# A hybrid decoder layer on one core: bulk elementwise work put on VectorE, and tiles laid over other memory in the FFN and embedding stages

## The chip, the cores and the metric

The kernel runs on one core of a Trainium2 chip. The metric is the device time of one execution in microseconds (us), the median of several runs. The core has a matrix engine (TensorE, PE in the profile), three engines for elementwise work (VectorE or DVE, ScalarE or ACT, GpSimd or POOL) and SyncE (SP), on whose queue this kernel issues its DMAs.

## The reference, cut to what matters

One layer of a decoder, over 1056 tokens (32 of the decoding samples, then 1024 of a prompt), width 1024, float32. Every half has a norm ahead of it and a norm behind it, whose result is added to the residual:

```python
x += 0.5 * post(swiglu_1(pre(x)))                 # FFN1, inner width 2816
cols = pre(x) @ w_in
x += post(concat(gdn(cols), swa(cols)) @ w_out)   # gated DeltaNet and sliding-window attention
x += 0.5 * post(swiglu_2(pre(x)))                 # FFN2
x += post(sigmoid(x @ ple_gate) * (p @ ple_proj)) # per-layer input embedding ("PLE")

def swiglu(h, w_gate, w_up, w_down):
    return (silu(h @ w_gate) * (h @ w_up)) @ w_down
```

It also returns the convolution and recurrent states and the attention caches.

## The kernel before, in words

**Precision.** Every float32 operand is split into a rounded half `hi` and a rest `lo = x - hi`; a product is three matmuls (hi·hi, hi·lo, lo·hi; `mm3`, lines 136 to 138, `mm3p`, lines 353 to 355). A split is a cast on ScalarE and a subtraction, which for weights is line 129 (128x1024, tile `wsp` from `raw`), on VectorE unless the caller passes `pl`, and then on GpSimd.

**Tiling.** Activations lie with features on the partitions (8 slices of 128) and tokens along a row, in three chunks `CH` of 288, 384 and 384 tokens. Weights come in 1 MB raw tiles, two buffers, are split into units and used once for every chunk.

**Stages.** Load and pre-norm (`apply_norm`, lines 217 to 227: scale, cast to `hi`, subtraction for `lo` at line 226, odd slices on GpSimd). FFN up (`ffn_up`): the first and last weight groups directly, the groups between by a scheme of seven products for chunks 1 and 2 together, whose token-side sums come from `half_sums` (lines 359 to 377): four steps `k`, each four additions on GpSimd (line 366), four on VectorE (368 to 371), and three splits (375, 376; the first on GpSimd). The SwiGLU output is written to memory tile by tile (`scr_h<-sg`, line 399), 22 tiles of 128 features for each chunk. FFN down (`ffn_down`): for each chunk `load_g` reads the 22 tiles back one at a time (line 538, tile `gr`, four buffers) and splits them to `gt` (539, 540); the matmuls run over them; a `Sum` (lines 192 to 211: square on ScalarE, addition on an engine of a list) gathers the norm; and `finish`, a generator, does the post-norm, residual (610, 611) and the next stage's `hi`/`lo` of the chunk before, two of its steps behind each weight unit. Then come the input projection, the recurrent and attention groups (the "mixer"), the output projection (`load_mix` reads the mixed tiles `xm` and gates `zz`), FFN2 in the same way with chunk order 1, 2, 0, and PLE: gate matmuls (lines 1719 to 1723, in the order chunks 1, 2, 0), input tiles `pin`, their transposes to `pT`, the projection units `upj`, and a norm with `gB`.

**What sets the order.** The program is written stage by stage, and a scheduler with priorities orders each engine's instructions; each engine then runs its queue strictly in that order, and SP issues the DMAs in its own. Memory comes from pools that are opened and closed: a pool opened after another closed lies over the same bytes, and its first writes wait for the last uses of what lay there. `fp` holds FFN up's own tiles (the sums `st`, `ut`, the outputs `sg`); it is closed ahead of the down stage, whose pools `yd` (one output tile of 8x384) and `gp` (`gt` and `gr`) lie there. In PLE, `pp`, `pr` and `pe` lie over these in turn; the fourth gate unit is `u3`.

## Time and profile before

| | |
|---|---|
| median of 3 runs | 2448.47 us (2448.35 to 2451.45) |
| the profiled execution | 2444.39 us |
| its span, first to last instruction | 2442.7 us |
| mean granted TensorE clock | 0.963 of full |
| PE busy | 2265.5 us (93%) |
| VectorE, ScalarE, GpSimd busy | 1422.3, 924.3, 294.0 us |

The profile is one execution. A row of a group reads: line, engine, operation, output tile from input tiles, shapes, count; then busy time and the mean of one in ns; then how long the engine stood idle before these instructions and which instruction ended that. A timeline row has the start, the length, the instruction, and in brackets the idle time before it with what ended it. In a row of windows the busy times of PE, weight loads, VectorE, ScalarE and GpSimd follow the window's length, then the granted clock, the share of the DMA engines and GB/s.

### The profile page before, as it was taken

To read this page: it belongs to the slowest core of one execution; us is meant where nothing else is said; L and a number is where in the kernel's file an instruction comes from. 1 tells how busy PE (TensorE), PEld (TensorE's weight loads), DVE (VectorE), ACT (ScalarE), POOL (GpSimd) and SP (SyncE) were. 2 spreads that over 40 slices of the span, in tenths; PEclk is the share of its full clock that TensorE was granted. 3 is DMA by queue.
4 is the path that set the end of the run, shared out by engine and by line. 5 is a ranking of instruction groups with operands and counts; after the bars stand their busy time and mean duration, and the time that the engine had idled before them with its cause. 6 is when DMAs were issued, how large, how long until landed. Compare 5 with 4: busy or idle time off the path is not lost. (4 is left out here: it accounts for less than half of the span.)

```text
span 2442.7 us, 36595 instructions
## 1 busy us (share of the span) xinstructions
PE 2265.5 (93%) x14212; PEld 2153.6 (88%) x14212; DVE 1422.3 (58%) x2839; ACT 924.3 (38%) x1862; POOL 294.0 (12%) x303
## 2 busy tenths in 40 slices
PE   6899999979999598879999989899999989999798
PEld 5899999979999597878887888799999989999576
DVE  6755555545774548891456668855555554655425
ACT  5322223335453335423326644322223234444221
POOL 2400000000000225332110333500000000001000
PEclk9999999989999798989999988999999999999799
DMA  6122222266554425646554544122222265554201
GB/s 230 57 77 91 75 83 75 83 211 207 195 193 130 128 67 190 180 132 191 176 178 123 150 164 165 48 75 83 75 83 73 85 207 182 188 169 142 96 16 57
DMA packets 312915, 313.17 MB, mean 128 GB/s; under 512 B 26185, under 2 KB 295569, under 8 KB 312726
## 3 DMA queue, kind: packets, MB, share of 16 engines
q1 hardware_dynamic: 312742, 310.84, 39.4%
q8 instruction: 112, 1.84, 0.3%
q14 instruction: 61, 0.50, 0.1%
HBM read 235.57 MB, written 77.81 MB: 128 GB/s over the span
## 5 line engine op out<-in xcount | busy, mean ns | idle before, releaser
L129 DVE TENSOR_TENSOR wsp<-raw,wsp 128x1024 fp32r<-128x1024 f32 (+1 forms) x271 | 325.9, 1203 | 266.2 <-ACT wsp L128 265.3
L128 ACT CAST wsp<-raw 128x1024 fp32r<-128x1024 f32 (+1 forms) x290 | 293.5, 1015 | 310.4 <-PE mm L355 178.7
L353 PE MATMUL mm<-gt,wsp 128*128 128x384 f32 (+1 forms) x1056 | 342.8, 326 | 24.1 <-ACT gt L539 10.2
L355 PE MATMUL mm<-gt,wsp 128*128 128x384 f32 (+1 forms) x1056 | 342.4, 325 | 2.9 <-DVE wsp L129 2.9
L354 PE MATMUL mm<-gt,wsp 128*128 128x384 f32 (+1 forms) x1056 | 342.7, 325 | 0.0
L136 PE MATMUL mm<-hhi,wsp 128*128 128x384 f32 (+1 forms) x784 | 265.6, 339 | 14.9 <-ACT po L767 10.8
L138 PE MATMUL mm<-hhi,wsp 128*128 128x384 f32 (+1 forms) x784 | 263.3, 336 | 4.0 <-DVE wsp L129 2.3
L137 PE MATMUL mm<-hlo,wsp 128*128 128x384 f32 (+1 forms) x784 | 263.8, 336 | 0.7 <-DVE hlo L226 0.5
L353 PEld LDWEIGHTS mm<-gt,wsp 128*128 128x128 f32 x1056 | 200.9, 191 | 26.6 <-ACT gt L539 20.8
L353 PE MATMUL ax<-hhi,wsp 128*128 128x384 f32 x640 | 215.5, 337 | 0.1
L355 PE MATMUL ax<-hhi,wsp 128*128 128x384 f32 x640 | 215.1, 336 | 0.2 <-DVE wsp L129 0.2
L354 PE MATMUL ax<-hlo,wsp 128*128 128x384 f32 x640 | 215.2, 336 | 0.0
L355 PEld LDWEIGHTS mm<-gt,wsp 128*128 128x128 f32 x1056 | 201.2, 191 | 4.3 <-DVE wsp L129 3.9
L354 PEld LDWEIGHTS mm<-gt,wsp 128*128 128x128 f32 x1056 | 201.2, 191 | 1.6 <-DVE gt L540 1.0
L128 ACT CAST wsp<-st 128x1024 fp32r<-128x1024 f32 x80 | 84.3, 1054 | 278.3 <-PE ax L355 272.0
L353 PE MATMUL ax<-th,wsp 128*128 128x384 f32 x480 | 161.7, 337 | 15.1 <-ACT th L375 15.1
L136 PEld LDWEIGHTS mm<-hhi,wsp 128*128 128x128 f32 x784 | 154.4, 197 | 19.1 <-ACT po L767 12.3
L353 PE MATMUL mm<-hhi,wsp 128*128 128x288 f32 x576 | 169.9, 295 | 0.1
L354 PE MATMUL mm<-hlo,wsp 128*128 128x288 f32 x576 | 169.8, 295 | 0.0
L355 PE MATMUL mm<-hhi,wsp 128*128 128x288 f32 x576 | 169.5, 294 | 0.0
L354 PE MATMUL ax<-th,wsp 128*128 128x384 f32 x480 | 161.6, 337 | 1.6 <-POOL th L376 1.6
L355 PE MATMUL ax<-th,wsp 128*128 128x384 f32 x480 | 160.9, 335 | 0.0
(461 smaller groups left out, 4696.8 us busy)
## 6 DMA issues: line engine op xcount, KB each, us to landing
raw<-in_ffn_w_down_dram SPq DMA_DIRECT2D x48, 1024.0 KB
raw<-in_ffn_w_gate_dram SPq DMA_DIRECT2D x24, 1024.0 KB
raw<-in_ffn_w_up_dram SPq DMA_DIRECT2D x24, 1024.0 KB
raw<-in_ffn_w_down_dram SPq DMA_DIRECT2D x24, 768.0 KB
scr_h<-sg SPq DMA_DIRECT2D x88, 192.0 KB
gr<-scr_h SPq DMA_DIRECT2D x88, 192.0 KB
raw<-in_w_out_dram SPq DMA_DIRECT2D x12, 1024.0 KB
xr<-scr_x SPq DMA_DIRECT2D x12, 768.0 KB
```

Source lines behind the costliest of these rows:

```text
L128: S.copy(hi, src)
L129: (G if pl else V).tensor_tensor(lo, src, hi.bitcast(F32), ALU.subtract)
L136: TE.matmul(ps, lhsT=wh, rhs=xh, start=(i == 0), stop=False)
L137: TE.matmul(ps, lhsT=wh, rhs=xl, start=False, stop=False)
L138: TE.matmul(ps, lhsT=wl, rhs=xh, start=False, stop=(i == n - 1))
L353: TE.matmul(ps, lhsT=wh, rhs=xh, start=(first and i == 0), stop=False, skip_group_check=on)
L354: TE.matmul(ps, lhsT=wh, rhs=xl, start=False, stop=False, skip_group_check=on)
L355: TE.matmul(ps, lhsT=wl, rhs=xh, start=False, stop=(last and i == n - 1), skip_group_check=on)
```

## The change

1. Every large GpSimd subtraction or addition goes to VectorE: the `pl` splits (line 129, 19 instructions), the split at 784 (4), the odd `lo` slices of 226 (24), 626 and 1630 (12 each), the mixed tiles' `lo` (1510, 24), the additions of `half_sums` (366, 32, and 376, 8), and GpSimd's share of `Sum` (209, 18): 153 instructions. GpSimd keeps small operations of the mixer.
2. A pool `fq`, opened ahead of `fp`, takes `st` and `ut`; so `yd` of the down stage lies over these and no longer over output tiles. The first chunk of each down stage reads its first tiles (10 of 288 tokens, 8 of 384) in one DMA into a `yd` tile `ga`.
3. In PLE the pool order is turned: `pe` (now `y0b`, `gB`, `y1`) comes first, so that `pp` and `pr` (with `u3`, `upj`, `pin`, `pT`) lie over `gt`/`gr`. The load of `gB` moves to the second half.
4. In FFN2 down, `finish` takes four steps behind each weight unit (`rate`), FFN1 two as before.

```diff
-        (G if pl else V).tensor_tensor(lo, src, hi.bitcast(F32), ALU.subtract)
+        V.tensor_tensor(lo, src, hi.bitcast(F32), ALU.subtract)
...
-            (G if d % 2 else V).tensor_tensor(lo[:, d, :], hf, hi[:, d, :].bitcast(F32), ALU.subtract)
+            tt(lo[:, d, :], hf, hi[:, d, :].bitcast(F32), ALU.subtract)
...
-        s2 = Sum(n, "x", (G, V)) if sq else None
+        s2 = Sum(n, "x", (V,)) if sq else None
...
-                G.tensor_tensor(t, f32(hh[:, q, :]), f32(ll[:, q, :]), ALU.add)
+                tt(t, f32(hh[:, q, :]), f32(ll[:, q, :]), ALU.add)
...
-                (V if i else G).tensor_tensor(T[i][:, 1, k, :], t, f32(T[i][:, 0, k, :]), ALU.subtract)
+                V.tensor_tensor(T[i][:, 1, k, :], t, f32(T[i][:, 0, k, :]), ALU.subtract)
...
-            s12, s34 = [fp.tile([P, 1024], F32, name=nm("st"), tag="st", bufs=2) for _ in range(2)]
+            s12, s34 = [fq.tile([P, 1024], F32, name=nm("st"), tag="st", bufs=2) for _ in range(2)]
...
+            na = 0
+            if c == order[0]:
+                na = KT * 384 // n
+                ga = wide([P, KT, 384], F32, name=nm("ga"), tag="yd", bufs=1).rearrange("p a b -> p (a b)")[:, :na * n]
+                ga = ga.rearrange("p (f n) -> p f n", n=n)
+                dma(ga, scr[:, 0:na, c0:c0 + n])
             for f in range(NF):
                 gt = gp.tile([P, 2, 384], F32R, name=nm("gt"), tag="gt")[:, :, :n]
-                gr = gp.tile([P, 384], F32, name=nm("gr"), tag="gr", bufs=4)[:, :n]
-                dma(gr, scr[:, f, c0:c0 + n])
+                if f < na:
+                    gr = ga[:, f, :]
+                else:
+                    gr = gp.tile([P, 384], F32, name=nm("gr"), tag="gr", bufs=4)[:, :n]
+                    dma(gr, scr[:, f, c0:c0 + n])
...
-                        next(prev, None)
-                        next(prev, None)
+                        for _ in range(rate):
+                            next(prev, None)
...
-            G.tensor_tensor(lo, src, hi.bitcast(F32), ALU.subtract)
+            tt(lo, src, hi.bitcast(F32), ALU.subtract)
...
-            G.tensor_tensor(lo[:, k, :], xm, hi[:, k, :].bitcast(F32), ALU.subtract)
+            tt(lo[:, k, :], xm, hi[:, k, :].bitcast(F32), ALU.subtract)
...
-        ss = Sum(n, "y", (G, V))
+        ss = Sum(n, "y", (V,))
...
-            (G if d % 2 else V).tensor_tensor(lo[:, d, :], y[:, d, :], f32(hi[:, d, :]), ALU.subtract)
+            V.tensor_tensor(lo[:, d, :], y[:, d, :], f32(hi[:, d, :]), ALU.subtract)
...
+        y0b = pe.tile([P, 3, 512], F32, name="y0b")
+        gB = pe.tile([P, D], F32, name="gB")
         u3 = pp.tile([P, 2, 1024], F32R, name=nm("wsp"), tag="wsp")
...
-        gB = pr.tile([P, D], F32, name="gB")
-        dma(gB, A["norm_ple_post"].broadcast_to([P, D]))
-        V.tensor_scalar(gB, gB, 0.5, None, op0=ALU.mult)
         y0a = pr.tile([P, 6, 512], F32, name="y0a")
-        y0b = pe.tile([P, 3, 512], F32, name="y0b")
...
                 us = gate_units(1)
+                dma(gB, A["norm_ple_post"].broadcast_to([P, D]))
+                V.tensor_scalar(gB, gB, 0.5, None, op0=ALU.mult)
...
-                    y = pr.tile([P, 512], F32, name=nm("y1"), tag="y1", bufs=2)[:m]
+                    y = pe.tile([P, 512], F32, name=nm("y1"), tag="y1", bufs=2)[:m]
...
-    with tc.tile_pool(name="pp", bufs=1) as pp, tc.tile_pool(name="pr", bufs=1) as pr, tc.tile_pool(name="pe", bufs=1) as pe:
+    with tc.tile_pool(name="pe", bufs=1) as pe, tc.tile_pool(name="pp", bufs=1) as pp, tc.tile_pool(name="pr", bufs=1) as pr:
```

The scheduler reacts to these edits with another order at three places that matter here. On PE, in the first half-sum stage before, the matmuls of two successive sets of sums (`th`, accumulating in one `ax` tile, rows of the same unit) stand close together:

```order
392 L353 MATMUL ax_927<-th_814,wsp_910 128x384
393 L354 MATMUL ax_927<-th_814,wsp_910 128x384
394 L355 MATMUL ax_927<-th_814,wsp_910 128x384
395 L353 MATMUL ax_927<-th_814,wsp_910 128x384
396 L353 MATMUL ax_928<-hhi_557,wsp_910 128x384
```

On PE after (the same place; lines 353 to 355 are unchanged, and `mm_1121` and `ax_1104` belong to the next unit, `wsp_1086`):

```order
396 L355 MATMUL ax_930<-th_817,wsp_913 128x384
397 L355 MATMUL ax_931<-hhi_560,wsp_913 128x384
...
401 L353 MATMUL ax_1104<-hhi_392,wsp_1086 128x384
...
428 L355 MATMUL mm_1121<-hhi_208,wsp_1086 128x288
429 L353 MATMUL ax_930<-th_817,wsp_913 128x384
```

Matmuls of the next unit, 12 into `ax` and 24 into `mm` in this stretch and its continuation, have moved ahead of the later `th` matmuls.

On SP at the end of FFN1 up, before (`raw` are weights of the down stage, `sg` the last output tiles, `xr` residuals):

```order
114 L556 DMA raw_4642<-in_ffn_w_down_dram 128x8x256
...
116 L399 DMA scr_h_89<-sg_4406 128x288
117 L556 DMA raw_4698<-in_ffn_w_down_dram 128x6x256
...
119 L399 DMA scr_h_89<-sg_4460 128x288
...
121 L538 DMA gr_4473<-scr_h_89 128x288
122 L538 DMA gr_4478<-scr_h_89 128x288
```

After (line 540 is the new load, 547 the `gr` load, 565 the weights):

```order
114 L540 DMA ga_4476<-scr_h_89 128x10x288
115 L399 DMA scr_h_89<-sg_4409 128x288
116 L565 DMA raw_4628<-in_ffn_w_down_dram 128x8x256
117 L565 DMA raw_4684<-in_ffn_w_down_dram 128x6x256
118 L399 DMA scr_h_89<-sg_4463 128x288
...
120 L547 DMA gr_4509<-scr_h_89 128x288
```

The new load stands ahead of the two last output tiles, and the weight load that stood ahead of them now stands between them.

On ScalarE at the start of PLE, before (`hhi` are the last chunk's `hi` slices, `wsp_21411` is `u3`):

```order
1512 L597 COPY rb_21364<-fx_21337 128x288
1513 L1629 CAST hhi_21382<-yd_20592 128x288 x8
1514 L128 CAST wsp_21411<-raw_21323 128x1024
1515 L128 CAST upj_21418<-raw_21416 128x1024
1516 L128 CAST upj_21421<-raw_21416 128x1024
```

After (`u3` is `wsp_21389`; line 606 was 597, 1641 was 1629):

```order
1513 L128 CAST wsp_21389<-raw_21299 128x1024
1514 L1685 CAST identr<-cx 128x128
1515 L128 CAST upj_21396<-raw_21394 128x1024
1516 L128 CAST upj_21399<-raw_21394 128x1024
1517 L606 COPY rb_21340<-fx_21313 128x288
1518 L1712 CAST pT<-ax_21409 128x384
...
1521 L1641 CAST hhi_21358<-yd_20568 128x288 x2
```

The fourth gate unit, the projection units and the first `pT` have moved ahead of the last chunk's `hi` slices.

More of the change, by code (lines that the diff above doesn't have):

```diff
@@ L375, in half_sums, with ffn_up @@
                 S.copy(T[i][:, 0, k, :], t)
-                (V if i else G).tensor_tensor(T[i][:, 1, k, :], t, f32(T[i][:, 0, k, :]), ALU.subtract)
+                V.tensor_tensor(T[i][:, 1, k, :], t, f32(T[i][:, 0, k, :]), ALU.subtract)
             yield
     SGB = 10
-    def ffn_up(H, wg, wu, fp, scr, order, opent, hooks={}):
+    def ffn_up(H, wg, wu, fq, fp, scr, order, opent, hooks={}):
         NG = F // 256
@@ L510, in tmp @@
                 def tmp(self):
-                    return fp.tile([P, 384], F32, name=nm("ut"), tag="ut", bufs=4)
+                    return fq.tile([P, 384], F32, name=nm("ut"), tag="ut", bufs=4)
                 def c0(self, j, ps):
@@ L526, in ffn_up, with ffn_down @@
             classic(0, NG - 1, j, ug, uu)
-    def ffn_down(wd, gp, scr, order, yt, finish, after):
+    def ffn_down(wd, gp, scr, order, yt, finish, after, wide, rate):
         NF = F // 128
@@ L625, in g_pre_norm @@
             S.copy(hi[:, d, :], hf)
-            (G if d % 2 else V).tensor_tensor(lo[:, d, :], hf, f32(hi[:, d, :]), ALU.subtract)
+            V.tensor_tensor(lo[:, d, :], hf, f32(hi[:, d, :]), ALU.subtract)
             yield
@@ L633, in emit @@
     scr_h = [dram.tile([P, F // 128, T], F32, name=f"scr_h{i}") for i in range(2)]
+    fqc = tc.tile_pool(name="fq", bufs=1)
+    fq = fqc.__enter__()
     fpc = tc.tile_pool(name="fp", bufs=2)
@@ L655, in nx @@
         return f
-    ffn_up(H, A["ffn1_w_gate"], A["ffn1_w_up"], fp, scr_h[0], (0, 1, 2), open_t, hooks={
+    ffn_up(H, A["ffn1_w_gate"], A["ffn1_w_up"], fq, fp, scr_h[0], (0, 1, 2), open_t, hooks={
         (0, -1): nx(0), (0, 0): nx(1, 0), (0, 1): nx(1, 2), (0, 3): nx(1), (0, 4): nx(2, 2, 0, 1, 2),
@@ L661, in emit @@
     fpc.__exit__(None, None, None)
+    fqc.__exit__(None, None, None)
     w_in = A["w_in"][0]
@@ L688, in emit @@
         ffn_down(A["ffn1_w_down"], gp, scr_h[0], (0, 1, 2), lambda c: yd.tile([P, KT, 384], F32, name="yd", tag="yd", bufs=1) if c == 2
-                 else big.tile([P, KT, 384], F32, name=nm("yd"), tag="b2")[:, :, :CH[c][1]], finish1, first_units)
+                 else big.tile([P, KT, 384], F32, name=nm("yd"), tag="b2")[:, :, :CH[c][1]], finish1, first_units, yd.tile, 2)
     MGT, MLE = cm[:, 0:128], cm[:, 128:256]
@@ L1649, in emit @@
     ycur[0] = None
-    with tc.tile_pool(name="fp2", bufs=2) as fp:
-        ffn_up(H2, A["ffn2_w_gate"], A["ffn2_w_up"], fp, scr_h[1], (1, 2, 0), open_t)
+    with tc.tile_pool(name="fq2", bufs=1) as fq, tc.tile_pool(name="fp2", bufs=2) as fp:
+        ffn_up(H2, A["ffn2_w_gate"], A["ffn2_w_up"], fq, fp, scr_h[1], (1, 2, 0), open_t)
         tpc.pop().__exit__(None, None, None)
@@ L1654, in emit @@
         ffn_down(A["ffn2_w_down"], gp, scr_h[1], (1, 2, 0), lambda c: big.tile([P, KT, 384], F32, name=nm("yd"), tag="b2") if c == 1
-                 else yd.tile([P, KT, 384], F32, name=nm("yd"), tag="yd", bufs=1)[:, :, :CH[c][1]], finish2, first_gates)
+                 else yd.tile([P, KT, 384], F32, name=nm("yd"), tag="yd", bufs=1)[:, :, :CH[c][1]], finish2, first_gates, yd.tile, 4)
     def ple(pp, pr, pe):
```

## The prediction, made before the changed kernel was run

> **What bounds the kernel now.** I read the page's busy times first, then the whole span cut into stages.
>
> ```profile
> PE 2265.5 (93%) x14212; PEld 2153.6 (88%) x14212; DVE 1422.3 (58%) x2839; ACT 924.3 (38%) x1862; POOL 294.0 (12%) x303
> ```
>
> TensorE (PE) is the bound: 2265.5 of 2442.7 us, so 177 us are idle. The matmuls themselves do not change, so only idle time, and matmuls run at a reduced clock, can be won. In the stages the columns are the busy time of PE, PEld, VectorE (DVE), ScalarE (ACT) and GpSimd (POOL), then the granted clock:
>
> ```profile
> 505.00:556.00 51.00, 37.97 (x250) 36.75 (x249) 21.29 (x35) 19.95 (x37) 0.00 (x0) 0.87 0.75 242
> 800.00:843.00 43.00, 18.29 (x98) 15.58 (x98) 29.46 (x69) 13.88 (x28) 10.51 (x10) 0.68 0.45 143
> 843.00:1270.00 427.00, 391.85 (x2843) 356.88 (x2842) 267.22 (x788) 163.19 (x502) 119.52 (x157) 0.96 0.51 157
> 1400.00:1560.00 160.00, 141.82 (x810) 136.55 (x809) 119.41 (x241) 72.24 (x135) 59.64 (x46) 0.91 0.46 152
> 1560.00:1585.00 25.00, 16.38 (x84) 14.78 (x84) 23.60 (x30) 9.05 (x18) 15.01 (x12) 0.80 0.02 7
> 2200.00:2300.00 100.00, 77.45 (x496) 72.16 (x495) 53.51 (x89) 37.51 (x61) 12.67 (x8) 0.83 0.43 142
> ```
>
> The loss sits at transitions: FFN1 up to down (13.0 us idle), FFN1 down to input projection (24.7), recurrent mixer (35.2 in 427), output projection (18.2), half-sums (8.6), FFN2 down to embedding (22.6). What PE waited for, with total, times and longest:
>
> ```profile
> PE ax L353 <- ACT th L375: 15.1, 4, 6.0
> PE mm L1719 <- ACT wsp L128: 12.3, 1, 12.3
> PE fx L172 <- DVE ss L209: 12.1, 5, 4.8
> PE ax L1056 <- DVE qk L1069: 12.0, 4, 6.4
> PE mm L136 <- ACT po L767: 10.8, 2, 10.1
> PE fx L582 <- DVE ss L209: 10.7, 3, 9.7
> PE mm L353 <- ACT gt L539: 10.2, 3, 7.8
> PE mm L353 <- DMA gr<-scr_h: 9.3, 1, 9.3
> PE mm L353 <- ACT yd L568: 3.4, 1, 3.4
> ```
>
> A wait costs more than itself. These windows lie on the matmuls right behind such waits, and the granted clock there is a half:
>
> ```profile
> 103.60:109.20 5.60, 5.60 (x17) 5.16 (x18) 5.02 (x10) 3.34 (x8) 1.85 (x2) 0.50 0.00 0
> 1569.20:1580.30 11.10, 6.23 (x17) 5.03 (x18) 11.10 (x14) 3.08 (x6) 7.56 (x6) 0.54 0.01 2
> 527.80:532.40 4.60, 4.60 (x19) 4.60 (x20) 3.01 (x7) 2.59 (x6) 0.00 (x0) 0.50 0.59 166
> 542.70:546.10 3.40, 3.40 (x16) 3.40 (x16) 0.80 (x3) 0.29 (x1) 0.00 (x0) 0.50 1.03 355
> 2288.50:2300.50 12.00, 9.55 (x25) 6.64 (x26) 5.19 (x6) 3.60 (x6) 0.00 (x0) 0.50 0.71 240
> ```
>
> Half of the busy time in such a window is lost: 2.8, 3.1, 2.3, 1.7 and 4.8 us.
>
> **The change part by part.** *The moved elementwise work.* 153 instructions leave GpSimd. What they took there, and the like of them on VectorE:
>
> ```profile
> L129 POOL TENSOR_TENSOR wsp<-raw,wsp 128x1024 fp32r<-128x1024 f32 x19 | 46.1, 2429 | 133.7 <-ACT wsp L128 133.7
> L366 POOL TENSOR_TENSOR hs<-hhi,hlo 128x384 f32<-128x384 f32 x32 | 39.9, 1269 | 15.9 <-DMA scr_h<-sg 10.3 <-DVE hs L369 2.9 <-DVE th L376 2.1
> L129 DVE TENSOR_TENSOR wsp<-raw,wsp 128x1024 fp32r<-128x1024 f32 x247 | 309.1, 1252 | 238.9 <-ACT wsp L128 238.2
> L209 DVE TENSOR_TENSOR ss<-ss,sq 128x384 f32<-128x384 f32 x58 | 33.6, 582 | 3.4 <-POOL ss L209 2.8 <-ACT sq L208 0.5
> L209 DVE TENSOR_TENSOR ss<-ss,sq 128x288 f32<-128x288 f32 x29 | 13.2, 454 | 9.4 <-ACT sq L208 7.5 <-POOL ss L209 1.9
> L376 DVE TENSOR_TENSOR th<-hs,th 128x384 fp32r<-128x384 f32 x16 | 14.8, 925 | 1.2 <-ACT th L375 1.2
> L368 DVE TENSOR_TENSOR hs<-hs,hs 128x384 f32<-128x384 f32 x8 | 9.3, 1156 | 0.0
> ```
>
> The added VectorE work is 23 wide splits by 1.25 = 29 us and 130 narrow ones by 0.45 to 0.58 = 59 to 75 us: about 96 us. Against it stands a relief: the same 128x384 operation takes 0.58 us in L209 but 0.93 and 1.16 us in L376 and L368, which run beside GpSimd. Plainest is this pair, two residual additions and two GpSimd splits:
>
> ```profile
> 806.62 5.39 DVE L611 TENSOR_TENSOR yd<-yd,xr 128x384 f32<-128x384 f32 x2
> 806.55 5.04 POOL L129 TENSOR_TENSOR wsp<-raw,wsp 128x1024 fp32r<-128x1024 f32 x2 [6.72 <-ACT wsp L128]
> ```
>
> Two additions worth 1.2 us took 5.39, ending as GpSimd did. The Trainium skill says the same (SBUF — State Buffer, Who interferes with whom): a VectorE instruction with two SBUF inputs and a GpSimd instruction reading SBUF hold a shared port in turn, and the second blocks fully. The trace agrees in this pair. The relief is bounded by zero and by the time GpSimd gives up, at most 294.0 us; I take 85 us, near the excess seen beside GpSimd, so VectorE's busy time hardly grows (1422 to about 1435) while a chain step drops from 1.3 to 2.4 us on GpSimd to 0.5 to 1.25 us.
>
> *Half-sums, twice.* The four steps feed PE through these two waits among others:
>
> ```profile
> 95.68 0.44 PE L353 MATMUL ax<-th,wsp 128*128 128x384 f32 x1 [1.23 <-ACT th L375]
> 103.56 0.69 PE L353 MATMUL ax<-th,wsp 128*128 128x384 f32 x1 [6.02 <-ACT th L375]
> ```
>
> A step takes 7.9 us now. On VectorE alone it is 12 operations by 0.58 = 7.0 us, so the last set arrives some 3 us earlier; and the changed order puts 36 matmuls of the next weight unit between the dependent ones (0.33 us each at half clock, so 0.165 by 36 = 5.9 us of work in the wait). Lost before in both stages: 15.1 idle and 5.9 by clock, 21.0. I leave 8, so 13 won (7 to 18). VectorE's queue behind it holds the next units' splits, which PE reaches only later.
>
> *First spilled tiles.* The first 10 of chunk 0 (8 of a 384 chunk) come as one DMA into memory that no longer lies over the last written tiles. But their casts write into the gp pool, which still does:
>
> ```profile
> 525.13 5.19 SPq L538 DMA_DIRECT2D gr<-scr_h  x8
> SPq L538 <- DMA scr_h<-sg: 4.7, 1, 4.7
> 527.80 0.85 PE L353 MATMUL mm<-gt,wsp 128*128 128x288 f32 x2 [9.28 <-DMA gr<-scr_h]
> 541.95 0.53 PE L353 MATMUL mm<-gt,wsp 128*128 128x288 f32 x2 [2.23 <-ACT gt L539]
> ```
>
> SP waited 4.7 us until the last spill had landed at 525.1; the matmul followed 2.7 us later. After the change the cast, no longer the load, waits for that landing, and the spill's DMA stands behind two weight loads and the new load (10 x 288 x 128 x 4 B = 1.47 MB). So the start moves only by about 2 us, to 525.6 to 526, and of the later refill stalls 2.23 us and 1.7 us of half clock go: 6.5 (4 to 9, more if the spill lands at 523). FFN2 lost 7.8 and some 2 by clock; 2.5 of it (0.5 to 5). Together 9 (3 to 20, the upper end if no cast waited).
>
> *Down to projection.* The 5.39 us pair shrinks to 1.2, but its two splits now sit ahead in VectorE's queue at 2.5: 1.7 earlier, and the odd halves of the pre-norm save about 2: 4 (0 to 8).
>
> *The embedding.*
>
> ```profile
> 2283.41 3.97 POOL L1630 TENSOR_TENSOR hlo<-yd,hhi 128x288 fp32r<-128x288 f32 x4 [67.31 <-ACT hhi L1629]
> 2274.76 1.22 PE L594 MATMUL fx<-dg,cx 128*128 128x256 f32 x2 [2.54 <-DVE dg L589]
> 2287.41 1.04 ACT L128 CAST wsp<-raw 128x1024 fp32r<-128x1024 f32 x1 [3.67 <-POOL hlo L1630]
> 2294.99 1.12 PE L1697 MATMUL ax<-cx,pin 128*128 128x128 f32 x4 [2.27 <-DMA pin<-in_p_prompt_dram]
> ```
>
> The fourth gate unit's memory lies over yd and waits for the last hlo; then the input tiles land late. After, it lies over the gt tiles, free once the last down matmul has run, which is ahead of the three gate units that PE does before its 12.3 us wait; and the gate matmuls of two chunks, which need nothing of the third, fill the gap. Lost: 12.3, 2.3, 2.5 for the diagonal, and 4.8 by clock: 22. Left are stalls for the diagonal, the landing and the pT split, which stands behind the norm on VectorE, about 7: 15 won (8 to 19). The gB load moves behind other input on SP and is first used in the second half: nothing.
>
> *Four steps per unit* in FFN2 down: the norm ends earlier; of the 3.4 us wait 2 go (-1 to 4).
>
> *Mixer and output projection, 843 to 1560.* The relief and the added work nearly cancel; the square sums of the output projection (12.1 us of waits) shorten by some 0.7 us for each GpSimd addition (1.27 against 0.58, as above), but the order also moves the loads of mixed tiles behind later spills. I take 3 (-15 to 12).
>
> Sum: 13 + 9 + 4 + 15 + 2 + 3 = 46. The profiled execution took 2444.4 us, of which 1.7 lie around the span; it comes to 2398. The median of the runs, 2448.5, is 4.1 above it, and I forecast against that: **2402**.
>
> On small waits a rule would speak: the 2.23 us at 541.95 is followed by 3.40 us at clock 0.50. The Trainium skill (TensorE: Matmul & The Clock Gate, Part 1) has the throttle come after an idle window of about 3.4 us, by which the stalls that I leave at 2 to 3 us would run on at full clock and the sum would be some 4 us larger; the row disagrees, and I go by the row.
>
> **The rivals.** *The maps bring little*: the casts still wait for the spill, and the embedding's inputs for their landing. For it speaks the 4.7 us wait above; against it that u3's releaser is the hlo by name. The 24 us of both shrink to 5: 2427.
>
> *The order of the mixer loses*: the first output projection chunk is not spread over the attention's tail any more, and its loads stand two at a time behind the last spills. Two buffers for eight tiles are four rounds, at the 2.7 us from the gr load to its matmul 11 us, and half as much again by clock: 16 off the 46, 2418 to 2430. For: the mixer already holds 35 us of idle time, so its order counts; against: the projection's z units fill the tail instead.
>
> *VectorE becomes the bound, slower*: if it stalls beside GpSimd for other reasons than GpSimd, the relief is zero and 96 us come on top. In 1560 to 1585 it is busy 23.6 of 25 us and in 1400 to 1560 119 of 160, so there the added microseconds show: 20 narrow operations in each half-sum stage, 12 us twice; the 46 GpSimd instructions of 1400 to 1560 by 0.5, 23; and of the mixer's 18 splits by 1.25, where it is busy 267 of 427, a quarter: 5. That is 52, against the 30 of the spilled tiles, projection, embedding and norm steps: 2470. It decides where the relief falls under some 40 us, since 52 less its share of 96 is then 30. Against it stands the 5.39 us pair. The Trainium skill (Perfetto Trace Analysis, Optimizing Scalar/DVE Operations) advises the other direction, work off a saturated VectorE even to GpSimd, with the reserve that the shared port may void it; the row favours the reserve.
>
> *More than forecast*: casts free early, and all half-clock windows at transitions go: the parts' upper ends, 18 + 20 + 8 + 19 + 4, and 5 of the mixer, 74 instead of 46, 2374.
>
> **How the numbers follow.** Forecast (2385 to 2418) 0.53; maps bring little 0.14; order loses 0.13; more than forecast 0.10; slower 0.08; around no change, where the losses just meet the gains, 0.02. The range 2380 to 2437 takes in the first three and part of the fourth, leaving out less than 2 in 10. About 0.2% (5 us) is what a measurement here can tell from no change: faster 0.90, same 0.02, slower 0.08.
>
> **What would show it.** Right: GpSimd busy under 100 us, VectorE 1400 to 1450; L376 and L368 near 0.58; the wait on ACT th under 6 us; the first down matmul 1 to 3 us sooner behind the last up matmul; no wait above 4 us on the gate matmuls; and fewer windows at clock 0.50. Wrong: VectorE above 1480, new waits of L172 or L1056 on it, or waits on xm loads near 1400.

## The result, and the profile after

The changed kernel takes 2367.2 us (median, 2363.7 to 2374.4), the kernel before 2449.3 us in the same comparison: a ratio of 0.9667, 95% interval 0.9644 to 0.9691, or 82 us less. The forecast had 46. The profiled executions are 2444.4 and 2367.4 us, 77 us apart; the other 5 us are there because the profiled execution of before lay that much under its median.

The page of the changed kernel has these busy times:

```profile
PE 2252.4 (95%) x14212; PEld 2142.4 (91%) x14212; DVE 1421.6 (60%) x2992; ACT 920.9 (39%) x1862; POOL 78.4 (3%) x150
```

GpSimd fell from 294.0 to 78.4 us. VectorE runs 153 more instructions and is busy no longer than before (1422.3). PE's idle time fell from 177 to 113 us, and its busy time by 13 us: the same 14212 matmuls ran at a mean granted clock of 0.975 instead of 0.963.

Cut at the same points of the program, the windows of before come first. The cuts are the first matmul of FFN1 down, the first of the input projection, its first after the wait for the conv tiles, the first with half-sum tiles in FFN2, the first of FFN2 down, and its last:

```profile
0.00:527.80 527.80, 490.34 (x3011) 481.28 (x3012) 297.53 (x460) 172.97 (x277) 39.44 (x38) 0.98 0.31 105
527.80:798.40 270.60, 264.45 (x1621) 260.99 (x1622) 162.08 (x286) 130.78 (x218) 9.10 (x8) 0.99 0.56 181
798.40:838.00 39.60, 14.89 (x90) 12.51 (x88) 29.80 (x69) 12.75 (x26) 10.81 (x10) 0.72 0.46 146
838.00:1564.80 726.80, 668.58 (x4602) 609.56 (x4603) 470.07 (x1244) 318.13 (x890) 200.43 (x225) 0.95 0.49 151
1564.80:1995.80 431.00, 414.59 (x2581) 412.57 (x2580) 237.95 (x338) 127.11 (x176) 11.53 (x10) 0.98 0.26 87
1995.80:2266.80 271.00, 262.77 (x1599) 258.77 (x1600) 146.21 (x226) 123.57 (x199) 13.73 (x8) 0.98 0.53 173
2266.80:2442.70 175.90, 149.83 (x715) 117.97 (x713) 78.66 (x222) 38.99 (x82) 8.92 (x6) 0.91 0.15 52
```

And of the changed kernel:

```profile
0.00:513.80 513.80, 486.64 (x3011) 478.83 (x3011) 295.48 (x492) 172.91 (x277) 0.31 (x5) 0.99 0.32 107
513.80:779.10 265.30, 261.87 (x1620) 259.20 (x1621) 161.64 (x294) 129.78 (x218) 0.00 (x0) 0.99 0.57 186
779.10:814.70 35.60, 16.72 (x91) 14.81 (x89) 28.25 (x74) 12.56 (x26) 1.63 (x4) 0.73 0.51 162
814.70:1526.30 711.60, 670.21 (x4601) 605.99 (x4602) 476.00 (x1327) 317.10 (x890) 76.45 (x141) 0.95 0.49 154
1526.30:1946.70 420.40, 413.18 (x2582) 411.91 (x2581) 235.02 (x348) 127.20 (x175) 0.00 (x0) 0.99 0.27 88
1946.70:2211.80 265.10, 259.39 (x1599) 257.10 (x1600) 145.87 (x234) 122.89 (x199) 0.00 (x0) 0.99 0.55 178
2211.80:2365.70 153.90, 144.33 (x715) 114.60 (x713) 79.36 (x228) 38.45 (x82) 0.00 (x0) 0.99 0.17 60
```

The differences of the lengths are the gains by stage, beside the forecast's terms:

| stage | gain, us | forecast for it |
|---|---|---|
| start, half-sums and up of FFN1, to its first down matmul | 14.0 | 8.5 (half of the half-sums' 13, and 2 of the spilled tiles) |
| FFN1 down | 5.3 | 4.5 (refill stalls) |
| wait ahead of the input projection | 4.0 | 4 |
| mixer and output projection | 15.2 | 3 |
| half-sums and up of FFN2, to its first down matmul | 10.6 | 8 |
| FFN2 down | 5.9 | 3 |
| embedding | 22.0 | 15 |
| sum | 77.0 | 46 |

The forecast gave the 2.5 us of FFN2's spilled tiles without a stage; here 1.5 stand ahead of its first down matmul and 1 behind it.

One profile is a rough measure of a stage. Kernels of this study whose code and order are the changed kernel's in a stage differ there by some 5 us up to the first down matmul (513.0 to 517.8), by 10 in the mixer and output projection (705 to 716) and by 4 in FFN2 down (265 to 270, two at 273 and 276 apart), so smaller differences of a stage are not read. The 15.2 us stand out of this all the same: the two kernels with the bulk work on GpSimd (before, and experiment 2) take 727 and 732 us in that stage. The 5.9 of FFN2 down do not.

What PE waits for now:

```profile
PE mm L138 <- DVE wsp L129: 10.6, 2, 9.9
PE mm L136 <- ACT po L779: 8.7, 1, 8.7
PE ax L1068 <- DVE qk L1081: 8.4, 6, 3.0
PE mm L353 <- ACT gt L548: 7.3, 1, 7.3
PE mm L353 <- DMA xr<-scr_x: 5.0, 1, 5.0
PE ax L353 <- ACT hhi L372: 3.8, 2, 2.2
PE mm L353 <- ACT yd L577: 2.3, 1, 2.3
PE mm L136 <- ACT pT L1712: 0.5, 1, 0.5
PE fx L172 <- DVE ss L209: 0.2, 1, 0.2
```

The waits for `th` (15.1) are gone, of the half-sums only 3.8 us on the neighbouring `hhi` are left; the square sums' 12.1 us are 0.2; the fourth gate unit's 12.3 us are gone. The large wait ahead of the projection has only changed its name: it was `ss` (9.7) and is now a weight split in VectorE's queue (9.9), with `po` behind it as before. VectorE's half-sum operations run at the same 0.55 us everywhere, where they took 0.93 and 1.16 us:

```profile
L366 DVE TENSOR_TENSOR hs<-hhi,hlo 128x384 f32<-128x384 f32 x32 | 16.1, 550 | 0.0
L376 DVE TENSOR_TENSOR th<-hs,th 128x384 fp32r<-128x384 f32 x24 | 13.1, 550 | 0.0
```

At the start of FFN1 down the timeline has, of SP, ScalarE and PE:

```profile
507.16 0.34 SPq L399 DMA_DIRECT2D scr_h<-sg  x1
513.35 3.43 ACT L548 CAST gt<-ga 128x288 fp32r<-128x288 f32 x10 [1.51 <-DMA scr_h<-sg]
513.84 0.85 PE L353 MATMUL mm<-gt,wsp 128*128 128x288 f32 x2 [7.25 <-ACT gt L548]
```

The last spilled tile is issued at 507.16 and lands at 513.3; the first cast waits for exactly that, although the load of its own data was issued at 495.38, and the first matmul follows 0.5 us after the landing (2.7 us before).

### The profile page after: what moved, and what is told of

Same layout as the page of the kernel before. It is cut to its first block, busy times and chain, and to the rows that moved or that the text cites. A ratio compares the mean times of both kernels' runs of the same rounds, so it can differ in the third digit from the quotient of the medians.

```text
span 2365.7 us, 36438 instructions
## 1 busy us (share of the span) xinstructions
PE 2252.4 (95%) x14212; PEld 2142.4 (91%) x14212; DVE 1421.6 (60%) x2992; ACT 920.9 (39%) x1862; POOL 78.4 (3%) x150
## 4 chain that ended last, share of the span: by engine, by line
PE 77%; DVE 13%; DMA 5%; ACT 3%; issue 2%; SPq 0%; DVEq 0%; ACTq 0%; POOL 0%; POOLq 0%
PE ax L353 8%; PE ax L354 8%; PE ax L355 8%; PE mm L353 8%; PE mm L355 8%; PE mm L354 8%; PE mm L136 5%; PE mm L137 5%; PE mm L138 5%; DMA gr<-scr_h 3%; PE mm L1735 1%; PE mm L1731 1%; PE mm L1732 1%; DVE cy L1026 1%; PE ax L986 1%
## 5 line engine op out<-in xcount | busy, mean ns | idle before, releaser
L129 DVE TENSOR_TENSOR wsp<-raw,wsp 128x1024 fp32r<-128x1024 f32 (+1 forms) x290 | 342.1, 1181 | 282.1 <-ACT wsp L128 281.0
L138 PEld LDWEIGHTS mm<-hhi,wsp 128*128 128x128 f32 x784 | 153.4, 196 | 15.9 <-DVE wsp L129 10.1
L136 PEld LDWEIGHTS mm<-hhi,wsp 128*128 128x128 f32 x784 | 153.7, 196 | 13.5 <-ACT po L779 9.5
L353 PE MATMUL ax<-th,wsp 128*128 128x384 f32 x480 | 161.1, 336 | 0.6 <-DVE sg L477 0.6
L354 PE MATMUL ax<-th,wsp 128*128 128x384 f32 x480 | 160.4, 334 | 0.0
```

What stands on the lines that cost most here:

```text
L129: V.tensor_tensor(lo, src, hi.bitcast(F32), ALU.subtract)
L136: TE.matmul(ps, lhsT=wh, rhs=xh, start=(i == 0), stop=False)
L138: TE.matmul(ps, lhsT=wl, rhs=xh, start=False, stop=(i == n - 1))
L353: TE.matmul(ps, lhsT=wh, rhs=xh, start=(first and i == 0), stop=False, skip_group_check=on)
L354: TE.matmul(ps, lhsT=wh, rhs=xl, start=False, stop=False, skip_group_check=on)
```

## The experiments

The theory after the comparison (A): the engine move and the maps gain separately, the engine move mostly because GpSimd no longer holds VectorE up while both read SBUF (L), and not only because a slow engine left the chains (H). Below, a cost against the changed kernel is the ratio's distance from 0.9665 (the changed kernel gave 0.9667 and, run again, 0.9663) times 2449 us; the intervals are about 0.0024 either way, 6 us, unless given otherwise.

**1. The engine move alone.**

```diff
 before.py
-        (G if pl else V).tensor_tensor(lo, src, hi.bitcast(F32), ALU.subtract)
+        V.tensor_tensor(lo, src, hi.bitcast(F32), ALU.subtract)
 (and the other bulk GpSimd operations likewise)
```

Expected: 

> The kernel before with the 153 bulk instructions moved to VectorE and nothing else: no early spilled tiles, the embedding's memory as it was, two finish steps per unit. Theory A (the gains of the engine move and of the maps are separate and add up; by the stages of the two traces the engine move brings half-sums 18, mixer with output projection 14, projection 4 and the start 2): about 2449 - 38 = 2411 us, the wait before the fourth gate unit still there but shorter by the GpSimd hlo. Rival B (what the forecast took: the engine move is worth 20 and the maps 24): about 2429. Rival C (the maps do nearly all): within 10 us of 2449.

Measured: 0.9796 (0.9769 to 0.9823), 50 us under the kernel before (43 to 57 by the interval). That is more than Theory A's 38, and far from the forecast's 20.

**2. The maps alone.**

```diff
 after.py
-        V.tensor_tensor(lo, src, hi.bitcast(F32), ALU.subtract)
+        (G if pl else V).tensor_tensor(lo, src, hi.bitcast(F32), ALU.subtract)
 (and the other bulk operations likewise)
-... finish2, first_gates, yd.tile, 4)
+... finish2, first_gates, yd.tile, 2)
```

Expected: 

> The maps alone: early load of the first spilled tiles and the turned pools of the embedding, all bulk work on GpSimd as before, two finish steps per unit. Theory A: spilled tiles 10 and embedding 20 to 22, so about 2449 - 31 = 2418 us. Rival B (as forecast, stalls of some 7 us left in the embedding and 9 for the tiles): 2425. Rival D (the gates' hlo on GpSimd holds the embedding whatever the map): 2440 or more.

Measured: 0.9868 (0.9842 to 0.9894), 32 us. With the 50 above it makes 82, which is what the whole change gained: the parts add up within their intervals, and rival D is out.

**3. The half-sums back on GpSimd**, twice.

```diff
-                tt(t, f32(hh[:, q, :]), f32(ll[:, q, :]), ALU.add)
+                G.tensor_tensor(t, f32(hh[:, q, :]), f32(ll[:, q, :]), ALU.add)
...
-                V.tensor_tensor(T[i][:, 1, k, :], t, ...
+                (V if i else G).tensor_tensor(T[i][:, 1, k, :], t, ...
```

Expected: 

> The changed kernel with only the half-sums' four additions and first split per step back on GpSimd (40 instructions of 153). Theory A: the two half-sum stages lose what they won, 16 to 19 us, about 2367 + 17 = 2384, with the waits on th back at 10 us or more in all. Rival B (the forecast's 13): 2380. Rival E (the stage was won by the other order on TensorE, which this kernel nearly keeps): under 5 us, 2372.

And of the second run: 

> The changed kernel with the half-sums back on GpSimd again, on the same chip: +18 to +24 us, 0.974 to 0.976.

Measured: 0.9754 (0.9733 to 0.9776) and 0.9742 (0.9719 to 0.9765), 22 and 19 us more than the changed kernel. The waits on `th` came back, in the second run:

```profile
PE ax L353 <- ACT th L375: 14.6, 4, 6.0
```

Rival E, the order on TensorE, is out, and the forecast's 13 was too small. Lined up matmul by matmul with the changed kernel, the two half-sum stages themselves (60 to 200 us and 1468 to 1650 us of its profile) are together 24 us longer in the first run and 21 in the second.

**4. GpSimd beside the half-sums, not in them.** GpSimd adds tiles that are already there into a tile that nobody reads; the results do not change, and the order on the other four engines is that of the changed kernel. The diff is of the kernel with eight additions in a step (3, 3 and 2 behind its three splits); the other has (2, 2, 1), five.

```diff
-    gains = cst.tile([P, 7, KT], F32, name="gains")
+    gains = cst.tile([P, 7, KT], F32, name="gains"); dump = cst.tile([P, 240], F32, name="dump")
...
-                V.tensor_tensor(T[i][:, 1, k, :], t, f32(T[i][:, 0, k, :]), ALU.subtract)
+                V.tensor_tensor(T[i][:, 1, k, :], t, f32(T[i][:, 0, k, :]), ALU.subtract); [G.tensor_tensor(dump, f32(T[i][:, 0, k, :240]), f32(T[i][:, 0, k, :240]), ALU.add) for _ in range((3, 3, 2)[i])]
```

Expected with eight additions in a step: 

> The changed kernel with eight more GpSimd additions (128x240, of th tiles into a tile that nobody reads) in each half-sum step; the output is the reference's, no result of GpSimd is waited for, and the order on the other four engines is that of the changed kernel. Theory L (the gain is VectorE freed from GpSimd, which holds it up while both read SBUF): VectorE's 128x384 operations of the stage rise from about 0.55 to 0.8 us or more and the time by 10 to 40 us. Rival H (the gain is only that the chain no longer passes through slow GpSimd instructions): under 3 us, VectorE's operations unchanged.

With five: 

> As the additions beside the half-sums, but five and not eight of them in each step, which is some 46 us of GpSimd time, about what the half-sums themselves had there (49). Against the kernel with the half-sums back on GpSimd (+21 to +24 us) it leaves out the chain through GpSimd and keeps the hold-up. Hold-up the larger part: +11 us or more. Chain the larger part: +8 us or less. Nothing of the hold-up: 0.

With five, run again: 

> The five additions per step beside the half-sums again. Hold-up the larger part of what the half-sums won: +11 us or more over the changed kernel (0.9663 of the kernel before), so 0.971 or more. Chain and order the larger part, as the stages of the trace say: +5 to +9 us, 0.968 to 0.970.

Measured: eight 0.9725 (0.9698 to 0.9752), 15 us more; five 0.9728 (0.9687 to 0.9768), 15 us more with an interval of 10 either way, then 0.9703 (0.9679 to 0.9726), 9 us more. Nothing waits for these additions, and yet VectorE's operations lengthen: with eight to 0.70 and 0.72 us (lines 366 and 376), short of the 0.8 expected, and with five, in the second run:

```profile
L366 DVE TENSOR_TENSOR hs<-hhi,hlo 128x384 f32<-128x384 f32 x32 | 17.3, 584 | 0.0
L376 DVE TENSOR_TENSOR th<-hs,th 128x384 fp32r<-128x384 f32 x24 | 15.7, 656 | 0.0
L376 POOL TENSOR_TENSOR dump<-th 128x240 f32<-128x240 f32 x40 | 64.4, 1610 | 401.4 <-ACT th L375 398.5
```

Rival H alone is out: VectorE is held up. How much of the half-sums' 19 to 22 us that is stays open. By the whole time five additions cost 15 of 22 us in one run and 9 of 19 in the other. By the stages it is less: lined up with the changed kernel matmul by matmul (the order on PE is the same), the two half-sum stages are about 6 us longer with five additions, in both runs, and 13 with eight, against 24 and 21 with the half-sums back. Both profiles with five are another 10 and 8 us longer in FFN2 down, where GpSimd does nothing and the code is the changed kernel's; in the second, PE is busy 4 us longer there, at a granted clock of 0.97 against 0.99, and the rest was not explained.

Nor is the dose that of the half-sums. The row's mean of 1.61 us is not a usual addition: half of them took 0.78 us or less, but one in each half-sum stage took 12.2 and 18.0 us (the last section shows it), so that most of the others came after the work that they were to disturb. The chain through GpSimd with its order was not tested by itself; that it takes the rest of the half-sums' loss is a subtraction.

**5. The square sums back on GpSimd** (every second addition of the mixer's norms).

```diff
-        s2 = Sum(n, "x", (V,)) if sq else None
+        s2 = Sum(n, "x", (G, V)) if sq else None
...
-        ss = Sum(n, "y", (V,))
+        ss = Sum(n, "y", (G, V))
```

Expected: 

> The changed kernel with GpSimd's share of the mixer's square sums back (18 additions, the rest on VectorE). By the traces projection, mixer and output projection together won 19 us where 7 were forecast. Theory S (the sums' chain sets the output projection's pace: its waits for the sums fell from 12.1 to 0.2 us): +8 to +14 us over the changed kernel, with 8 us or more of waits for ss again. Rival L2 (no single chain, but any bulk GpSimd work that holds VectorE, in proportion to its time; the sums are 25 of some 133 us there): +3 to +4.

Measured: 0.9722 (0.9697 to 0.9746), 14 us more, and the waits are there again:

```profile
PE fx L172 <- DVE ss L209: 9.1, 5, 4.2
```

The output projection, from PE's first matmul on a mixed tile to FFN2's first, in the changed kernel and then in this one:

```profile
1344.60:1467.50 122.90, 112.81 (x661) 105.76 (x660) 95.55 (x213) 71.00 (x144) 0.00 (x0) 0.94 0.58 191
```

```profile
1343.20:1475.30 132.10, 115.41 (x663) 108.91 (x662) 99.68 (x204) 70.75 (x143) 23.18 (x15) 0.92 0.57 183
```

It is 9.2 us longer, while six other profiles of the changed code there take 122.6 to 123.7 us. Theory S holds, and L2's 3 to 4 us are out. Another 4 us of its profile lie ahead of FFN1 down, where this kernel is the changed one, so the size of the whole is uncertain by that much.

**6. GpSimd beside the output projection.**

```diff
-                ss.add(y[:, d, :])
+                ss.add(y[:, d, :]); d and [G.tensor_tensor(dump, y[:, d, :240], y[:, d, :240], ALU.add) for _ in range(2)]
```

Expected: 

> The changed kernel with two GpSimd additions (128x240, of an output tile into a tile that nobody reads) behind each square sum of the output projection, 42 in all; the output is the reference's and the order on the other four engines is that of the changed kernel. Theory L (VectorE held up while both read SBUF): +5 to +15 us, with VectorE's additions of the sums above 0.6 us and waits for ss back. Rival H (only the chain through GpSimd counts): under 2 us.

Measured: 0.9731 (0.9708 to 0.9754), 16 us more. The output projection between the same two matmuls as in experiment 5, and a wait that the changed kernel has at 0.2 us:

```profile
1346.30:1481.10 134.80, 117.30 (x661) 109.61 (x660) 108.21 (x216) 72.83 (x144) 33.11 (x40) 0.91 0.55 179
PE fx L172 <- DVE ss L209: 6.2, 4, 3.0
```

The square sums in that stretch, in the changed kernel and then in this one:

```profile
L209 DVE TENSOR_TENSOR ss<-ss,sq 128x384 f32<-128x384 f32 x28 | 15.1, 551 | 0.7 <-ACT sq L208 0.6
```

```profile
L209 DVE TENSOR_TENSOR ss<-ss,sq 128x384 f32<-128x384 f32 x28 | 17.6, 638 | 0.5 <-ACT sq L208 0.4
```

GpSimd's group in the same kernel:

```profile
L1540 POOL TENSOR_TENSOR dump<-y 128x240 f32<-128x240 f32 x42 | 34.5, 822 | 234.2 <-DMA xm<-scr_mix 154.3 <-ACT y L1539 78.1
```

With 33 us of GpSimd beside it, VectorE needs 108.2 us for what took it 95.6, and the stretch is 12 us longer (122.9 in the changed kernel). So here the hold-up goes straight into the time: theory L.

**7. The wide splits back on GpSimd.**

```diff
-        V.tensor_tensor(lo, src, hi.bitcast(F32), ALU.subtract)
+        (G if pl else V).tensor_tensor(lo, src, hi.bitcast(F32), ALU.subtract)
...
-            tt(lo, src, hi.bitcast(F32), ALU.subtract)
+            G.tensor_tensor(lo, src, hi.bitcast(F32), ALU.subtract)
```

Expected: 

> The changed kernel with the wide splits back on GpSimd (19 weight splits and the 4 of the attention projection, 57 us of GpSimd time, nearly all in the projection and the mixer). Theory S: the mixer is set by its own chains, so 0 to +5 us. Rival L2 (in proportion): +7 to +10. Rival Q (VectorE's queue is full in the mixer's solve, so taking 29 us of splits off it helps): faster, -2 to -6.

Measured: 0.9711 (0.9687 to 0.9736), 11 us more, which is over theory S's 5 and near the 7 to 10 of L2. Rival Q, that VectorE's full queue would gain, is out; the page shows why:

```profile
PE 2248.3 (95%) x14212; PEld 2141.0 (90%) x14212; DVE 1423.6 (60%) x2969; ACT 922.2 (39%) x1862; POOL 132.9 (6%) x173
```

VectorE has 23 wide splits (28 us at 1.23) less to do and is busy 2 us longer than in the changed kernel.

**8. The mixed tiles' lo back on GpSimd.**

```diff
-            tt(lo[:, k, :], xm, hi[:, k, :].bitcast(F32), ALU.subtract)
+            G.tensor_tensor(lo[:, k, :], xm, hi[:, k, :].bitcast(F32), ALU.subtract)
```

Expected: 

> The changed kernel with the 24 mixed tiles' lo back on GpSimd (24.6 us there). Theory L (GpSimd holds VectorE up by some 0.3 us per us of its own in the output projection, as measured with additions beside it): +4 to +9 us, VectorE's busy time there up by 3 us or more. Rival H (only chains through GpSimd count, and these lie ahead of their use): under 2 us; or faster by 1 to 3, with 13 us taken off VectorE's queue.

Measured: 0.9692 (0.9662 to 0.9721), 7 us more with an interval that reaches zero: not decided by time.

```profile
PE 2250.1 (95%) x14212; PEld 2140.4 (90%) x14212; DVE 1418.7 (60%) x2968; ACT 920.3 (39%) x1862; POOL 107.7 (5%) x174
```

VectorE's busy time fell by 2.9 us for 24 operations (11 to 13 us at 0.45 to 0.55) that it no longer does. Of what it was spared three quarters came back as hold-up. In the output projection the square sums of 128x384 rise to 0.67 us and the waits for `ss` to 4.2, but the stretch takes 123.6 us, against 122.9: there the hold-up cost next to no time.

**9. The embedding's pools as before.**

```diff
-    with tc.tile_pool(name="pe", ...) as pe, tc.tile_pool(name="pp", ...) as pp, tc.tile_pool(name="pr", ...) as pr:
+    with tc.tile_pool(name="pp", ...) as pp, tc.tile_pool(name="pr", ...) as pr, tc.tile_pool(name="pe", ...) as pe:
 (gB, y0b, y1 and the load of gB as before)
```

Expected: 

> The changed kernel with the embedding's pools in the old order (pp, pr, pe), so that the fourth gate unit and the input tiles lie over yd again; the last chunk's hlo stays on VectorE. Theory A (the map alone closed the gap, and nothing of the 7 us of leftover stalls that were forecast exists): +17 to +21 us, the wait before the fourth gate unit back at 10 us or more. Forecast's size: +12. Rival (the hlo off GpSimd did it): under 5.

Measured: 0.9730 (0.9714 to 0.9746), 16 us more, with an interval of 4 either way; in its trace the embedding is 20 us longer than in the changed kernel. The wait ahead of the fourth gate unit is back:

```profile
PE mm L1731 <- ACT wsp L128: 11.2, 1, 11.2
```

The map did it, not the hlo's engine.

**10. Every spilled tile read by itself.**

```diff
-            if c == order[0]:
+            if False:
```

Expected: 

> The changed kernel with every spilled tile read one at a time as before; the pool fq stays. Forecast's step (the start of FFN1 down gains 2 us, its refill stalls 4, FFN2 2.5): +9 us, refill waits on gt back. Theory A (by the traces of the engine move alone and of the whole change, 13 us in FFN1 down): +12 to +15. Rival (the tiles are hidden behind the spill anyway): under 4.

Measured: 0.9713 (0.9697 to 0.9730), 12 us more.

```profile
PE mm L353 <- ACT gt L548: 10.7, 3, 8.2
PE mm L353 <- DMA gr<-scr_h: 10.4, 1, 10.4
```

21 us of waits ahead of down matmuls, against 12.3 in the changed kernel (7.3 on `gt`, and 5.0 that its list puts down to a residual load). The forecast's 9 and the 12 cannot be told apart.

**11. The last spilled tiles from ScalarE's queue.**

```diff
-            dma(scr[:, f, CH[c][0]:CH[c][0] + CH[c][1]], sg)
+            (nc.scalar.dma_start if c == 0 and f >= F // 128 - 2 else dma)(scr[:, f, CH[c][0]:CH[c][0] + CH[c][1]], sg)
```

Expected: 

> The changed kernel with the last two spilled tiles of each FFN written by a DMA from ScalarE's queue, so that they do not stand behind 1.8 MB of weights on SP's. After the change the first cast of the down stage waits for the landing of the last of them, 6.2 us after its issue. If that queue sets the landing: it lands 2 to 3 us after its issue, the first wait of the down stage falls from 7.3 to 3 to 5 us, and the time by 3 to 8 us in both FFNs together. If the sixteen DMA engines are shared in order whatever the queue: no change, within 2 us.

Measured: 0.9669 (0.9647 to 0.9691), no change.

```profile
512.11 0.33 ACTq L399 DMA_DIRECT2D scr_h<-sg  x1
518.61 1.76 ACT L548 CAST gt<-ga 128x288 fp32r<-128x288 f32 x5 [5.53 <-DMA scr_h<-sg]
```

It took 6.5 us from issue to landing, as from SP's queue (6.2), and it was issued 5 us later than from SP (507.16), behind a cast on ScalarE that waited for weights until 512.03. The DMA engines were full with SP's loads meanwhile (a share of 0.90 to 1.06 from 508 to 516 us), by then also with residuals, issued from 510.45. So this spill landed no sooner for being on another queue; what it would do if issued as early as from SP is not shown.

**12. Two finish steps per unit.**

```diff
-... finish2, first_gates, yd.tile, 4)
+... finish2, first_gates, yd.tile, 2)
```

Expected: 

> The changed kernel with two finish steps per unit in FFN2 down instead of four. The second down stage won 5.9 us by the traces, and 2 were forecast for the rate. Theory A (the rate brings the rest): +4 us. Rival (the stage was won by VectorE freed of GpSimd and by the early tiles; the rate is worth nothing): within 1.5 us of the changed kernel.

Measured: 0.9668 (0.9642 to 0.9694). The rate is worth nothing that can be measured.

**13. The mixer's other GpSimd multiplications on VectorE too.**

```diff
-        G.tensor_tensor(v4(gD), MLE.unsqueeze(1).broadcast_to([P, 4, 128]), bc(gg[:, n + 1, :], 128), ALU.mult)
+        V.tensor_tensor(v4(gD), MLE.unsqueeze(1).broadcast_to([P, 4, 128]), bc(gg[:, n + 1, :], 128), ALU.mult)
 (and the same for kd, qh, the samples' kd and qd, s_ and vx)
```

Expected: 

> The changed kernel with the mixer's remaining GpSimd multiplications (some 35 instructions of 128x512, 32x512 and 128x1024, about 48 us of GpSimd) on VectorE too. If the hold-up and the slow chain bind there as well: 5 to 15 us faster than the changed kernel. If VectorE's full queue in the solve is the bound: some 20 us of added work come out as +5 to +15 us. If they cancel: within 4 us.

Measured: 0.9625 (0.9589 to 0.9661), overlapping the changed kernel's interval. So both were run in five rounds on one chip.

Expected of the changed kernel: 

> The changed kernel once more, as the other side of the next run: 0.965 to 0.969 of the kernel before.

And of the other: 

> The kernel with the mixer's GpSimd multiplications on VectorE again, beside the changed kernel on the same chip. If the hold-up binds in the mixer too, 5 us or more below the changed kernel, outside both intervals; if the first run was chance, within 3 us.

Measured: 0.9663 (0.9640 to 0.9687) and 0.9615 (0.9596 to 0.9635), medians 2366.7 and 2352.9 us: 12 us by the ratios, the intervals just apart. Busy times of the changed kernel in this run, then of this one:

```profile
PE 2251.2 (95%) x14212; PEld 2140.8 (91%) x14212; DVE 1421.9 (60%) x2992; ACT 921.3 (39%) x1862; POOL 78.5 (3%) x150
```

```profile
PE 2248.4 (95%) x14212; PEld 2141.0 (91%) x14212; DVE 1426.7 (60%) x3030; ACT 922.5 (39%) x1862; POOL 37.0 (2%) x112
```

GpSimd gives up 41 us and VectorE takes 38 instructions for 5 us. That is the best version of this study. Which part of the 12 us is hold-up and which the shorter chain was not separated.

## Why the prediction was right in direction and wrong in size

**The direction and most mechanisms held.** VectorE at 1435 and GpSimd under 100 us were forecast; 1421.6 and 78.4 came. The slower rival rested on a relief under 40 us, and the relief paid for all of the added work, some 96 us, where 85 had been taken. At FFN1 down the forecast's chain happened step by step: the cast waits for the last spill, the matmul follows it at once. The wait ahead of the projection gave the 4 us forecast, but not quite as written: the two splits stand not ahead of the residual additions but behind them, at 796.64 and 798.25 us, and the first of them is the wait that is left.

**Where the 36 us lie.** The engine move by itself gave 50 us, where its terms (13, 4 and 3) make 20; the maps gave 32, where theirs (9 and 15) make 24; the rate gave nothing, where 2 were taken.

**The step that failed first** is the one on the mixer and output projection: "The relief and the added work nearly cancel ... I take 3." They did cancel, in busy time (470.1 us before, 476.0 after in that stage), and the stage still gained 15.2 us. Busy time was the wrong measure. What GpSimd held up were the operations that PE was about to wait for, square sums and split tiles, and what VectorE took over is done there in half the time. Experiments 5 and 6 show both: sums back on GpSimd lengthen the output projection by 9 us with the old waits, and GpSimd work beside them, waited for by nobody, by 12. The 12.1 us wait for the sums, which the forecast quoted, should have been priced as a wait that goes. That the hold-up costs time is shown; that it is the larger part of the engine move's 50 us is not. The four parts put back one by one (experiments 3, 5, 7 and 8) cost 51 to 54 us, each with an interval of about 6; the odd `lo` slices (48 of the 153 instructions) were not put back by themselves.

**Leftover stalls that were not there.** In the embedding "about 7" were left for the diagonal, the input tiles' landing and the pT split; the trace has 0.5 and 0.2 us, so the whole 22 us went (the map alone 16 to 20, experiment 9). The forecast let the gate matmuls of two chunks fill the 12.3 us, but not these stalls; in the trace they stand between the diagonal, the input tiles and the projection, and fill these too. In the half-sums 8 were left and 13 taken: experiment 3 has 19 to 22, the waits left are 3.8 us, and the granted clock of FFN1's stage is 1.00 (60 to 130 us), where it was 0.93. Both are the right mechanism with a term set too small.

**Smaller terms.** The spilled tiles at 9 measured 12 (not to be told apart). The rate at 2 measured 0. FFN2 down gained 5.9 us all the same; no experiment isolates that, and with the spread of the same code there (265 to 270 us) it may be 1 to 6. The start, taken at nothing, won some 2 us by its stage, which is within what one profile can tell. And 5 of the 36 us are in no stage: the gain was counted from the profiled execution of before, which by chance lay that much under its median. Two sums are off by their own terms: the rival of the maps comes to 2421 (46 less 19), not 2427, and the parts of FFN1's first tiles (2, 2.23 and 1.7) to 5.9, not 6.5. Neither decides anything.

The rival "more than forecast" had the time (2374) but not the reason: its casts were to be free early, and they were not. The advice of the Trainium skill that speaks against this change (Perfetto Trace Analysis, Optimizing Scalar/DVE Operations: take work off a saturated VectorE, "even GPSIMD") was tested from the other side by experiments 7 and 8: putting work back on GpSimd freed VectorE of nothing (2 us more) or little (2.9 us less). The reserve stated there, that with the shared port it might not help, is what these two runs agree with.

## What to carry to other kernels

Before giving VectorE's elementwise work to GpSimd, compare VectorE's busy time with and without it: here its gain was zero, and each chain step through GpSimd was about twice as long (1.27 against 0.55 us, 2.43 against 1.22). Price such a move by the waits that stand behind the operations held up, not by busy time. And when a gap is filled with independent matmuls, count those matmuls before leaving stalls in the sum.

## What the runs showed of the hardware that was not expected

The hold-up goes both ways, and it can last. In experiment 4, second run with five, the additions of GpSimd took (shortest, median and longest, in ns):

```profile
L376 POOL TENSOR_TENSOR dump<-th x40: 587/782/18046, 85.2 to 1556.8; 128x240 f32<-128x240 f32 x40
1520.17 18.05 POOL L376 TENSOR_TENSOR dump<-th 128x240 f32<-128x240 f32 x1 [309.60 <-ACT th L375]
1520.20:1538.20 18.00, 15.96 (x105) 15.28 (x103) 17.97 (x37) 6.95 (x13) 18.00 (x1) 1.00 0.00 1
```

The longest stretches over a time in which VectorE runs 37 operations without a gap, nearly all of them half-sums with both inputs in SBUF, and VectorE is not slowed by it. It ends where VectorE's run has its first gap, 0.03 us at 1537.80. From then on both engines go on, and VectorE's operations of the same shape take 0.93 us:

```profile
1537.22 0.55 DVE L369 TENSOR_TENSOR hs<-hs,hs 128x384 f32<-128x384 f32 x1
1538.56 0.94 DVE L370 TENSOR_TENSOR hs<-hs,hs 128x384 f32<-128x384 f32 x1
```

All three profiles of experiment 4 have such an addition of 18 us. The profile's times of GpSimd are rough, but VectorE's times change at the same moment.

The half clock does not follow the length of the wait alone. In the changed kernel a wait of 2.15 us has a window at half clock on it and one of 2.33 us has none:

```profile
1539.53 0.69 PE L353 MATMUL ax<-hhi,wsp 128*128 128x384 f32 x1 [2.15 <-ACT hhi L372]
2161.53 0.40 PE L353 MATMUL mm<-gt,wsp 128*128 128x288 f32 x1 [2.33 <-ACT yd L577]
```

```profile
1539.40:1542.70 3.30, 3.17 (x10) 3.08 (x11) 3.30 (x7) 1.99 (x6) 0.00 (x0) 0.50 0.00 0
2161.50:2164.90 3.40, 3.37 (x25) 3.37 (x26) 2.59 (x4) 2.00 (x4) 0.00 (x0) 1.00 0.39 127
```

So a wait of about 2 us costs itself or nearly twice itself (2.15 and half of 3.17 us), and which of them cannot be read off beforehand here. The Trainium skill (TensorE: Matmul & The Clock Gate, Part 1) has a free-running window of about 3.4 us, and a halved clock after an idle one. The 3.3 us row agrees with the length, and the two rows with an outcome that depends on where a wait falls; that a whole window must be idle they do not bear out.
